# Second MLP product in blocks: four column blocks from eleven loads with one seven-product half, or from fourteen products

## The chip, the cores and the metric

One core of one Trainium2 chip. The metric is device microseconds for one execution of the whole program, the median of three runs. Weights lie in HBM as float32 and are read once or more per execution; activations stay in the core's SBUF.

## The reference

Two pre-norm residual layers over 256 tokens of width 2048: a Mamba-2 mixer in the first, dilated window attention in the second, and after each a squared-ReLU MLP of width 8192. A final RMSNorm ends it. The part that the change touches is the MLP:

```python
def sq_relu_mlp(h, w1, w2):
    a = jax.nn.relu(h @ w1)
    return (a * a) @ w2
...
        x = x + sq_relu_mlp(rms_norm(x, norm_mlp[i]), mlp_w1[i], mlp_w2[i])
```

## The kernel before, in words

Everything is float32 to the outside. TensorE (PE) is fed in a rounded type (fp32r), so each operand is carried as a high and a low part, and a product is made of three matmuls: high by high, high by low, low by high. Weights come in units of 128 x 2048 float32 (1 MB). For each unit `fetch` (L160) loads the raw tile on SP's queue (L174), ScalarE (ACT) writes the high part `wh` (L187), and VectorE (DVE) writes the low part `wl` as raw minus high (L188). This pair is called a split below. `unit_plan` writes the order of all units by hand; `take` hands a unit to the product that wants it and fetches ahead: `LOOKAHEAD = 3` units and three buffers each of raw, `wh` and `wl`. A buffer of `wh` is free again when PE has ended the unit three places before. Within the MLP each split is issued after the split of the unit before it in the plan.

The MLP works through the 8192 hidden columns in eight chunks of 1024 (`FC = 8`). A chunk has eight w1 units, U0 to U7, of 32 matmuls each (L215, tile names h). Each is evacuated: ACT copies half of the PSUM bank, DVE adds the other half, applies the ReLU with the norm's factor (L777), ACT squares and makes the high part, DVE the low part (L780). While chunk c+1's U units run, the products of chunk c with w2 run between them, in the order of `CHUNK_ORDER` (L69), for the first seven chunks of each layer:

- Output columns 0 to 1023 are made with seven block products instead of eight (P1 to P7, L812, 12 matmuls of 512 columns each; tile names px, pw, pz for their PSUM banks). Each needs a sum of up to four weight blocks and a sum of activation blocks. The weight sums grow in two scratch tiles, wa (P1, P5, P6, P4) and wb (P3, P7): the first block is loaded, each later one is added to the tile by a DMA that accumulates, issued on GpSimd's (POOL's) queue (L176). The activation sums are made by `combine` on DVE and split (L791, L792). After each product DVE adds the bank to the residual or subtracts it (L818).
- Output columns 1024 to 2047 are made plainly: four units D20, D21, D30, D31 of 24 matmuls each (L249 to L251), added to the residual on DVE (L256).

The last chunk of each layer is made plainly for all columns.

The order of instructions on PE is that of the plan in this stage. On the other engines and on the DMA queues a scheduler, called by the kernel, orders instructions by when they become ready on its own timeline, within the orders that the kernel gives. A transfer on SP's queue thus need not stand in the plan's order.

Of the kernel before, what the change touches and what calls it, by code (L numbers as in the profile page):

```python
# [8 lines left out]
F32 = mybir.dt.float32  # L9
# [29 lines left out]
LOOKAHEAD = 3  # L39
# [7 lines left out]
def unit_plan():  # L47
# [21 lines left out]
CHUNK_ORDER = ("U0 U1 P1 U2 P2 U3 U4 P5 D20 D21 P3 U5 U6 P6 U7 D30 P7 D31 P4").split()  # L69
# [3 lines left out]
WINOGRAD = {  # L73
    "P1": ("wa", 0, 0, True), "P2": ("raw", 1, 0, True), "P5": ("wa", 0, 1, False),
    "P3": ("wb", 1, 1, True), "P6": ("wa", 1, 1, False), "P7": ("wb", 0, 1, False),
    "P4": ("wa", 1, 0, False),
# [3 lines left out]
def mlp_plan(layer):  # L80
    plan = [("w1", layer, 0, u) for u in range(8)]
    for c in range(FC):
        if c + 1 < FC:
            for item in CHUNK_ORDER:
                if item[0] == "U":
                    plan.append(("w1", layer, c + 1, int(item[1])))
                elif item[0] == "P":
                    plan.append(("w2", layer, c, item))
                else:
                    plan.append(("w2", layer, c, int(item[1]), int(item[2])))  # L90
        else:
            plan += [("w2", layer, c, j, q) for j in range(4) for q in range(2)]
    return plan
# [3 lines left out]
def hybrid_trunk_kernel(ctx: ExitStack, tc: tile.TileContext, a: dict, out: bass.AP):  # L97
# [7 lines left out]

    def mm_bank(name):
        return psum.tile([P, 512], F32, tag="mm", name=name, bufs=4)

    def sm_bank(name):
        return psum.tile([P, 512], F32, tag="sm", name=name, bufs=4)  # L110
# [20 lines left out]
    mlp_pool, sums_of = [None], {}  # L131
# [3 lines left out]
    def source(u):  # L135
# [15 lines left out]
        if len(u) == 4:  # L151
            q, j = WINOGRAD[u[3]][1:3]
        else:
            j, q = u[3:]
        return a["w2"][((u[1] * FC + u[2]) * 4 + j) * 2 + q], 2048

    def fetch(i, ends=(16,)):

        src, n = source(plan[i])
        product = plan[i][3] if plan[i][0] == "w2" and len(plan[i]) == 4 else None  # L160
        where, _, _, begins = WINOGRAD.get(product, ("raw", 0, 0, True))
        if where == "raw":
            raw = wts.tile([P, 2048], F32, tag="raw", name=f"raw{i}", bufs=3)
        elif begins:
            raw = sums_of[where] = mlp_pool[0].tile([P, 2048], F32, tag=where, name=f"{where}{i}", bufs=1)
        else:
            raw = sums_of[where]
        wh = wts.tile([P, 2048], F32R, tag="wh", name=f"wh{i}", bufs=3)
        wl = wts.tile([P, 2048], F32R, tag="wl", name=f"wl{i}", bufs=3)
        ready[i] = (wh, wl)  # L170
        for k0, k1 in zip((0, *ends), ends):
            c = slice(k0 * n // 16, k1 * n // 16)
            if begins:
                load[i] = nc.sync.dma_start(raw[:, c], src[:, c]).ins  # L174
            else:
                nc.gpsimd.dma_start(raw[:, c], src[:, c], accum_op=ALU.add)  # L176
            with ExitStack() as order:
# [3 lines left out]
                if product == "P4":  # L181
# [10 lines left out]
    def take(*u):  # L192
# [9 lines left out]
    def cols_units(us, xs, names, cuts=(), first=False, between=None):  # L202
# [3 lines left out]
        banks = [mm_bank(name) for name in names]  # L206
# [24 lines left out]
    def cols_sum(ps, name):  # L231
        cross = work.tile([P, S], F32, tag="cross", name=name + "x", bufs=2)
        nc.scalar.activation(cross, ps[:, S:], AF.Copy)
        tot = work.tile([P, S], F32, tag="tot", name=name + "t", bufs=2)
# [91 lines left out]
    def ssm(nx):  # L326
        sp = ctx_ssm.enter_context(tc.tile_pool(name="ssm", bufs=1))
# [312 lines left out]
    def attention(xn, nx):  # L640
        ap = ctx_att.enter_context(tc.tile_pool(name="att", bufs=1))
# [110 lines left out]
    def mlp(layer, pool, xn, done):  # L752
# [9 lines left out]
        mlp_pool[0] = pool  # L762

# [4 lines left out]
        def chunk(c):  # L768
            act = pool.tile([P, 8, 2, S], F32R, tag="act", name=f"act{layer}_{c}", bufs=2)
            r = pool.tile([P, 8, S], F32, tag="r", name=f"r{layer}_{c}", bufs=1)  # L770
            return act, r

        def evacuate(c, u, ps, act, r):
            name = f"h{layer}_{c}_{u}"
            tot = cols_sum(ps, name)
            t = r[:, u]
            nc.vector.scalar_tensor_tensor(t, tot, 0.0, rb, op0=ALU.max, op1=ALU.mult)  # L777
            nc.scalar.activation(t, t, AF.Square)  # L778
            nc.scalar.activation(act[:, u, 0, :], t, AF.Copy)
            nc.vector.tensor_tensor(act[:, u, 1, :], t, act[:, u, 0, :].bitcast(F32), ALU.subtract)  # L780

        def combine(c, r):

            t1, t2 = slice(0, P), slice(P, S)
            a11, a12, a21, a22 = r[:, :4, t1], r[:, 4:, t1], r[:, :4, t2], r[:, 4:, t2]
            s = [pool.tile([P, 4, P], F32, tag="s", name=f"s{layer}_{c}_{k}", bufs=2) for k in range(2)]
            parts = {}

            def split(k, t):
                parts[k] = pool.tile([P, 4, 2, P], F32R, tag=f"s{k}", name=f"sp{layer}_{c}_{k}", bufs=1)  # L790
                nc.scalar.activation(parts[k][:, :, 0], t, AF.Copy)  # L791
                nc.vector.tensor_tensor(parts[k][:, :, 1], t, parts[k][:, :, 0].bitcast(F32), ALU.subtract)  # L792

            nc.vector.tensor_tensor(s[0], a21, a22, ALU.subtract)
            split(1, s[0])
            nc.vector.scalar_tensor_tensor(s[1], s[0], -1.0, a11, op0=ALU.mult, op1=ALU.subtract)
            split(2, s[1])
            s4 = pool.tile([P, 4, P], F32, tag="s", name=f"s{layer}_{c}_3", bufs=2)
            nc.vector.scalar_tensor_tensor(s4, a12, -1.0, s[1], op0=ALU.mult, op1=ALU.subtract)
            split(4, s4)  # L800
            s3 = pool.tile([P, 4, P], F32, tag="s", name=f"s{layer}_{c}_2", bufs=2)
            nc.vector.tensor_tensor(s3, a11, a21, ALU.add)
            split(3, s3)
            return parts
# [11 lines left out]
        def put(m, j, ps, op):  # L816
            xc = x_res[:, m, j * 512:(j + 1) * 512]
            nc.vector.tensor_tensor(xc, xc, ps, op)  # L818

        act, r = chunk(0)  # L820
        us, names = [("w1", layer, 0, u) for u in range(8)], [f"h{layer}_0_{u}" for u in range(8)]
        for u, ps in enumerate(cols_many(us, xs, names)):
            evacuate(0, u, ps, act, r)

        for c in range(FC - 1):
            parts = combine(c, r)
            act_next, r_next = chunk(c + 1)
            banks = {}

            def half(k0, t):  # L830
                return lambda i, part: act[:, k0 + i, part, t]

            t1, t2 = slice(0, P), slice(P, S)
            of = {"P1": half(0, t1), "P2": half(4, t1), "P4": half(4, t2)}
            for k, item in ((1, "P5"), (2, "P6"), (3, "P7"), (4, "P3")):
                of[item] = lambda i, part, k=k: parts[k][:, i, part]
            lhs = lambda k, part, t: act[:, k, part, t]
            for item in CHUNK_ORDER:
                if item[0] == "U":
                    u = int(item[1])  # L840
                    ps = in_order(lambda: cols_units([("w1", layer, c + 1, u)], xs,
                                                     [f"h{layer}_{c + 1}_{u}"], first=(u == 0))[0])
                    evacuate(c + 1, u, ps, act_next, r_next)
                elif item[0] == "D":
                    j, q = int(item[1]), int(item[2])
                    if q == 0:
                        banks[j] = [mm_bank(f"d{layer}_{c}_{j}_{m}") for m in range(NH)]
                    in_order(lambda: rows_unit(banks[j], [("w2", layer, c, j, q)], lhs, 4 * q, 4, 512,
                                               q == 0, q == 1))
                    if q == 1:  # L850
                        add_residual(banks[j], j)
                else:
                    where = {"P1": "x", "P6": "x", "P7": "x", "P4": "x", "P5": "w", "P3": "w",
                             "P2": "z"}[item]
                    first = where not in banks
                    if first:
                        banks[where] = sm_bank(f"p{where}{layer}_{c}")
                    product(c, item, banks[where], of[item], first)
                    for m, j, op in {"P1": [(0, 0, ALU.add)], "P2": [(0, 0, ALU.add)],
                                     "P5": [(1, 1, ALU.add)], "P3": [(0, 1, ALU.subtract)],  # L860
                                     "P6": [(0, 1, ALU.subtract)], "P7": [(1, 1, ALU.add)],
                                     "P4": [(1, 0, ALU.subtract)]}[item]:
                        put(m, j, banks[where], op)
            act, r = act_next, r_next

        c = FC - 1
        lhs = lambda k, part, t: act[:, k, part, t]
# [18 lines left out]
    with tc.tile_pool(name="mlp1", bufs=1) as pool:  # L886
# [5 lines left out]
        def gained(j):  # L892
            if j == 0:
                fin.append(pool.tile([P, D], F32, tag="wb", name="fin", bufs=1))
# [116 lines left out]
```

## Time and profile before

| | us |
|---|---|
| median of 3 runs (2599.93 to 2601.69) | 2600.74 |
| the profiled execution | 2599.4 |
| its span | 2597.6 |

| engine | busy us | share of the span |
|---|---|---|
| PE | 2582.3 | 99% |
| PE weight load (beside PE) | 2211.8 | 85% |
| DVE | 1878.7 | 72% |
| ACT | 1459.1 | 56% |
| POOL | 160.0 | 6% |

Busy times are shares of an average over stages; the seven chunk steps of each layer are one such stage. "DMA share" is the mean busy share of the core's 16 DMA engines in a stretch, and GB/s what they moved. The releaser behind an arrow (`<-`) is the instruction that ended an engine's idle time.

### The profile page before, as it was taken

To read this page: it belongs to the slowest core of one execution; us is meant where nothing else is said; L and a number is where in the kernel's file an instruction comes from. 1 tells how busy PE (TensorE), PEld (TensorE's weight loads), DVE (VectorE), ACT (ScalarE), POOL (GpSimd) and SP (SyncE) were. 2 spreads that over 40 slices of the span, in tenths; PEclk is the share of its full clock that TensorE was granted. 3 is DMA by queue.
4 is the path that set the end of the run, shared out by engine and by line. 5 is a ranking of instruction groups with operands and counts; after the bars stand their busy time and mean duration, and the time that the engine had idled before them with its cause. 6 is when DMAs were issued, how large, how long until landed. Compare 5 with 4: busy or idle time off the path is not lost.

```text
span 2597.6 us, 34416 instructions
## 1 busy us (share of the span) xinstructions
PE 2582.3 (99%) x13977; PEld 2211.8 (85%) x13977; DVE 1878.7 (72%) x2182; ACT 1459.1 (56%) x1774; POOL 160.0 (6%) x131
## 2 busy tenths in 40 slices
PE   9999999999999999999999999999999999999998
PEld 7888888888888888888888999998888888888887
DVE  7888688686677677777766666666667777677765
ACT  7675365464555555555546655656565555555554
POOL 0121021211000000000000000000000000000001
PEclk9999999999999999999999999999999999999999
DMA  7645555555577787778765454444457777877783
GB/s 284 209 169 193 191 195 180 180 191 187 191 222 232 236 231 239 229 235 234 231 195 183 166 175 162 159 158 165 168 209 216 234 237 235 232 230 239 228 241 131
DMA packets 79087, 533.88 MB, mean 206 GB/s; under 512 B 8784, under 2 KB 9424, under 8 KB 19536
## 3 DMA queue, kind: packets, MB, share of 16 engines
q1 hardware_dynamic: 68256, 462.86, 50.5%
q0 software_dynamic: 8064, 58.72, 12.5%
q10 hardware_dynamic: 2608, 10.09, 1.2%
q8 instruction: 110, 1.80, 0.3%
q14 instruction: 49, 0.40, 0.0%
HBM read 529.48 MB, written 2.16 MB: 205 GB/s over the span
## 4 chain that ended last, share of the span: by engine, by line
PE 95%; DVE 2%; ACT 1%; DMA 1%; POOL 1%; issue 1%; SPq 0%; ACTq 0%; POOLq 0%; DVEq 0%
PE h L215 28%; PE qk L215 10%; PE c L215 8%; PE px L812 6%; PE d L249 5%; PE d L250 5%; PE d L251 5%; PE pw L812 3%; PE wo L250 2%; PE wo L249 2%; PE wo L251 2%; PE z L250 2%; PE z L251 2%; PE z L249 2%; PE v L249 2%; PE v L251 2%
## 5 line engine op out<-in xcount | busy, mean ns | idle before, releaser
L188 DVE TENSOR_TENSOR wl<-raw,wh 128x2048 fp32r<-128x2048 f32 (+4 forms) x428 | 934.6, 2185 | 578.0 <-ACT wh L187 577.0
L187 ACT ACTIVATE wh<-raw 128x2048 fp32r<-128x2048 f32 (+4 forms) x428 | 782.7, 1831 | 640.8 <-PE h L215 216.5
L215 PE MATMUL h<-xn,wh 128*128 128x512 f32 x2048 | 715.9, 394 | 0.0
L215 PE MATMUL h<-xn,wl 128*128 128x256 f32 x2048 | 571.2, 280 | 0.0
L215 PEld LDWEIGHTS h<-xn,wh 128*128 128x128 f32 x2048 | 383.9, 188 | 87.0
L215 PEld LDWEIGHTS h<-xn,wl 128*128 128x128 f32 x2048 | 383.6, 187 | 4.2
L215 PE MATMUL c<-xn,wh 128*128 128x512 f32 x768 | 272.4, 397 | 2.5 <-ACT wh L187 2.3
L215 PE MATMUL qk<-xn,wh 128*128 128x512 f32 x768 | 271.1, 395 | 0.0
L251 PE MATMUL d<-wh,act 128*128 128x512 f32 x576 | 224.3, 390 | 0.0
L250 PE MATMUL d<-wl,act 128*128 128x512 f32 x576 | 223.9, 389 | 0.0
L249 PE MATMUL d<-wh,act 128*128 128x512 f32 x576 | 218.7, 390 | 0.0
L215 PE MATMUL qk<-xn,wl 128*128 128x256 f32 x768 | 216.7, 284 | 0.0
L215 PE MATMUL c<-xn,wl 128*128 128x256 f32 x768 | 215.0, 282 | 0.8 <-DVE wl L188 0.8
L215 PEld LDWEIGHTS c<-xn,wh 128*128 128x128 f32 x768 | 143.7, 188 | 37.2 <-ACT wh L187 4.4
L215 PEld LDWEIGHTS qk<-xn,wh 128*128 128x128 f32 x768 | 143.9, 188 | 30.2
L215 PEld LDWEIGHTS c<-xn,wl 128*128 128x128 f32 x768 | 143.9, 188 | 3.0 <-DVE wl L188 1.1
L215 PEld LDWEIGHTS qk<-xn,wl 128*128 128x128 f32 x768 | 143.7, 188 | 3.2 <-issue 2.7
L251 PEld LDWEIGHTS d<-wh,act 128*128 128x128 f32 x576 | 108.1, 188 | 22.6
L249 PEld LDWEIGHTS d<-wh,act 128*128 128x128 f32 x576 | 108.1, 188 | 22.3
L250 PEld LDWEIGHTS d<-wl,act 128*128 128x128 f32 x576 | 108.1, 188 | 22.0
L778 ACT ACTIVATE r<-r 128x256 f32<-128x256 f32 x128 | 52.2, 410 | 101.7 <-DVE r L777 101.7
L250 PE MATMUL z<-wl,xn 128*128 128x512 f32 x256 | 101.4, 396 | 0.3 <-DVE wl L188 0.3
(348 smaller groups left out, 4186.3 us busy)
## 6 DMA issues: line engine op xcount, KB each, us to landing
raw<-in_w SPq DMA_DIRECT2D x214, 1024.0 KB, 4.9
raw<-in_w_in SPq DMA_DIRECT2D x74, 1024.0 KB, 4.8
raw<-in_w_qk SPq DMA_DIRECT2D x48, 1024.0 KB, 4.8
wa<-in_w POOLq DMA_DIRECT2D x42, 1024.0 KB, 8.2
raw<-in_w_out SPq DMA_DIRECT2D x32, 1024.0 KB, 4.8
raw<-in_w_v SPq DMA_DIRECT2D x32, 768.0 KB, 4.3
wa<-in_w SPq DMA_DIRECT2D x14, 1024.0 KB, 4.8
wb<-in_w SPq DMA_DIRECT2D x14, 1024.0 KB, 5.0
```

Source lines behind the costliest of these rows:

```text
L187: high[i] = nc.scalar.activation(wh[:, c], raw[:, c], AF.Copy).ins
L188: low[i] = nc.vector.tensor_tensor(wl[:, c], raw[:, c], wh[:, c].bitcast(F32), ALU.subtract).ins
L215: latest[0] = nc.tensor.matmul(ps[:, :n], (wh, wl)[part][:, kt * P:(kt + 1) * P], xs[:, kt, :, :].rearrange("p a t -> p (a t)")[:, :n], st ...
L249: nc.tensor.matmul(banks[m][:, :n], hi, wh[:, c], start=st, stop=False)
L250: nc.tensor.matmul(banks[m][:, :n], hi, wl[:, c], start=False, stop=False)
L251: latest[0] = nc.tensor.matmul(banks[m][:, :n], lo, wh[:, c], start=False, stop=sp).ins
L778: nc.scalar.activation(t, t, AF.Square)
L812: latest[0] = nc.tensor.matmul(ps, lhs(i, part), w[:, n], start=(first and i == 0 and part == 0 and w is wh), stop=(i == 3 and part == 1), ...
```

## The change

Both column halves are made from seven products. The four D units of a chunk go, and the seven products exist twice, a for columns 0 to 1023 and b for columns 1024 to 2047: fourteen products beside the eight U units. The order keeps U units apart; products stand next to each other in places.

```diff
-CHUNK_ORDER = ("U0 U1 P1 U2 P2 U3 U4 P5 D20 D21 P3 U5 U6 P6 U7 D30 P7 D31 P4").split()
+CHUNK_ORDER = ("1a U0 1b U1 5a U2 5b 3a U3 3b U4 6a U5 6b 7a U6 7b 2a 4a U7 2b 4b").split()
...
+PRODUCTS = {
+    "1": ("A", 0, 0, "load"), "5": ("A", 0, 1, "add"), "6": ("A", 1, 1, "add"), "4": ("A", 1, 0, "sum"),
+    "3": ("B", 1, 1, "load"), "7": ("B", 0, 1, "add"), "2": ("raw", 1, 0, "load"),
 }
```

A and B are the weight scratches, now Aa, Ab, Ba, Bb. "load" is a plain load, "add" an accumulating DMA. Product 4 has no DMA of its own: the block of product 2 is loaded for product 2, and DVE adds it to A, 128 x 2048, before product 4's split.

```diff
+                if item and item[0] == "2":
+                    a = sums_of["A" + item[1]]
+                    nc.vector.tensor_tensor(a[:, c], a[:, c], raw[:, c], ALU.add)
```

Buffers are named one by one instead of drawn from pools of three or four; the least recently used one is taken. In the chunk steps there are four pairs of `wh` and `wl` (three elsewhere), two raw buffers (three elsewhere; the third is Aa), and the fetch runs as far ahead as a free pair allows, three units.

```diff
+    banks_of, raws, splits = Slots(8), Slots(3), Slots(4)
...
+    def split_slot(i):
+        return splits.peek(range(4 if chunked(i) else 3))
...
-        while cursor[1] < min(len(plan), i + LOOKAHEAD):
+        while cursor[1] < len(plan) and splits.user.get(split_slot(cursor[1]), -1) < i:
```

PSUM banks are named as well: U units use banks 0, 1 and 6; the products banks 2, 3, 4, 5 and 7. Products 1, 6, 7, 4 share a bank (x) and 5, 3 share one (w), so each must wait until DVE has read the one before; product 2b shares a bank with 3b. Product 2a keeps bank 7 over all seven chunks and is added to the residual once, in the last. Outside the MLP the two groups of four banks stay, each bank now taken in fixed rotation.

```diff
+        put = {"1": ("x", 0, 0, ALU.add), "6": ("x", 0, 1, ALU.subtract), "7": ("x", 1, 1, ALU.add),
+               "4": ("x", 1, 0, ALU.subtract), "5": ("w", 1, 1, ALU.add), "3": ("w", 0, 1, ALU.subtract),
+               "2": ("z", 0, 0, ALU.add)}
+        place = {"wa": 2, "wb": 3, "xa": 4, "xb": 5, "za": 7, "zb": 3}
```

The activation sums are the same four per chunk, in three scratches (one of them a constant tile used elsewhere), each split once and used for both halves; the high and low parts of the left upper block and of the lower half lie in tiles of their own (`a1`, `a2`). The right upper block is split only in the last chunk (`complete`). The two reads of a U bank have priority over other work. The descriptor memory of POOL's DMAs is set to 4096 bytes.

## Rows read from the trace of the kernel before

**Rows 1.** The page: busy time of the engines over the span, and the granted clock of PE in 40 slices.

```profile
PE 2582.3 (99%) x13977; PEld 2211.8 (85%) x13977; DVE 1878.7 (72%) x2182; ACT 1459.1 (56%) x1774; POOL 160.0 (6%) x131
...
PEclk9999999999999999999999999999999999999999
```

**Rows 2.** The page: the chain of work that ended last, shares of the span by engine.

```profile
PE 95%; DVE 2%; ACT 1%; DMA 1%; POOL 1%; issue 1%; SPq 0%; ACTq 0%; POOLq 0%; DVEq 0%
```

**Rows 3.** The chain of waits in order of time, one chunk step of each layer (start us, length us, what).

```profile
945.26 2.75 PE pw L812 x12
961.61 11.17 PE h L215 x64
972.78 2.75 PE px L812 x12
975.53 5.59 PE h L215 x32
...
1979.37 2.75 PE pw L812 x12
...
2064.98 2.75 PE pw L812 x12
```

**Rows 4.** Busy time of each engine in four successive chunk steps of the first layer, each from one P5 to the next (columns: PE, PE weight load, DVE, ACT, POOL, with instructions; granted clock; DMA share; GB/s).

```profile
859.65:945.26 85.61, 85.61 (x437) 72.91 (x437) 62.52 (x62) 46.79 (x48) 3.43 (x4) 1.00 0.79 234
945.26:1030.88 85.62, 85.62 (x438) 72.91 (x437) 62.53 (x62) 46.80 (x48) 3.45 (x4) 1.00 0.79 233
1030.88:1116.49 85.61, 85.61 (x437) 72.90 (x437) 62.53 (x62) 46.78 (x48) 3.45 (x4) 1.00 0.79 234
1116.49:1202.10 85.61, 85.61 (x437) 72.90 (x437) 62.53 (x62) 46.79 (x48) 3.45 (x4) 1.00 0.78 234
```

**Rows 5.** Groups of DVE and ACT instructions in one chunk step, 945.26 to 1030.88 (count | busy us, mean ns of one | idle before them and its releaser).

```profile
L188 DVE TENSOR_TENSOR wl<-raw,wh 128x2048 fp32r<-128x2048 f32 x13 | 29.8, 2291 | 20.5 <-ACT wh L187 20.5
L780 DVE TENSOR_TENSOR act<-r,act 128x256 fp32r<-128x256 f32 x8 | 3.3, 418 | 0.0
L792 DVE TENSOR_TENSOR sp<-s,sp 128x512 fp32r<-128x512 f32 x4 | 2.7, 685 | 0.0
L818 DVE TENSOR_TENSOR x_res<-x_res,px 128x512 f32<-128x512 f32 x4 | 2.7, 679 | 0.0
...
L187 ACT ACTIVATE wh<-raw 128x2048 fp32r<-128x2048 f32 x14 | 26.8, 1917 | 25.3 <-PE h L215 13.1 <-PE d L251 8.9 <-issue 2.9
```

**Rows 6.** One split and the product that it feeds: ACT's and DVE's rows from the timeline, PE's from the chain.

```profile
1033.66 1.92 ACT L187 ACTIVATE wh<-wb 128x2048 fp32r<-128x2048 f32 x1 [0.38 <-PE pw L812]
...
1036.22 2.28 DVE L188 TENSOR_TENSOR wl<-wb,wh 128x2048 fp32r<-128x2048 f32 x1
...
1044.51 2.72 PE pw L812 x12
```

**Rows 7.** The DMA view of the same chunk step as rows 5: queues (packets, MB, share of 16 engines' time).

```profile
q1 hardware_dynamic: 2160, 15.73, 51.9%
q0 software_dynamic: 574, 4.18, 26.8%
```

**Rows 8.** Transfers about one accumulating DMA: its issue on POOL, the issue of a load on SP, the time to landing of both, and that of a load with no accumulating DMA beside it, issued at 985.3.

```profile
1003.50 0.86 POOL L176 DMA_DIRECT2D wa<-in_w  x1 [36.38 <-DVE wl L188]
...
L174 SPq DMA_DIRECT2D raw<-in_w x1: 328/328/328, 1007.3 to 1007.3; - x1
...
wa<-in_w POOLq DMA_DIRECT2D x1, 1024.0 KB, 8.2
raw<-in_w SPq DMA_DIRECT2D x1, 1024.0 KB, 6.6
...
L174 SPq DMA_DIRECT2D raw<-in_w x1: 328/328/328, 985.3 to 985.3; - x1
DMA to landing us min/median/max: 4.7/4.7/4.7
```

**Rows 9.** Stretches of the same few us (columns as in rows 4).

```profile
1005.00:1007.00 2.00, 2.00 (x14) 1.74 (x13) 2.00 (x1) 0.71 (x2) 0.00 (x0) 1.00 0.90 131
1007.00:1008.50 1.50, 1.50 (x11) 1.32 (x10) 1.50 (x4) 0.00 (x0) 0.00 (x0) 1.00 1.13 235
1008.50:1011.00 2.50, 2.50 (x14) 2.04 (x13) 0.48 (x2) 2.41 (x3) 0.00 (x0) 1.00 0.93 213
1011.00:1013.00 2.00, 2.00 (x13) 1.74 (x12) 2.00 (x2) 1.97 (x3) 0.00 (x0) 1.00 1.01 426
```

**Rows 10.** Issues on SP's queue before the U0 that starts the next chunk step at 997.47 (start us, length us).

```profile
980.48 0.33 SPq L174 DMA_DIRECT2D wb<-in_w  x1
985.31 0.33 SPq L174 DMA_DIRECT2D raw<-in_w  x1
990.89 0.33 SPq L174 DMA_DIRECT2D wa<-in_w  x1
...
997.47 11.16 PE h L215 x64
```

**Rows 11.** Who waited for whom in the attention stage, 1400 to 1880 us, the rows in which PE's side waits longest (us in total, times, longest us).

```profile
PEld qk L215 <- issue: 2.7, 7, 0.4
PEld pv L732 <- ACT ka L699: 1.7, 7, 0.2
```

More of the change, by code (lines that the diff above doesn't have):

```diff
@@ L86, in mlp_plan @@
                     plan.append(("w1", layer, c + 1, int(item[1])))
-                elif item[0] == "P":
+                else:
                     plan.append(("w2", layer, c, item))
-                else:
-                    plan.append(("w2", layer, c, int(item[1]), int(item[2])))
         else:
@@ L104, in hybrid_trunk_kernel, with __init__, peek, use @@
     dram = ctx.enter_context(tc.tile_pool(name="dram", bufs=1, space=bass.MemoryType.DRAM))
+    class Slots:
+        def __init__(self, n):
+            self.order, self.user = list(range(n)), {}
+        def peek(self, among):
+            return next(k for k in self.order if k in among)
+        def use(self, k, i=None):
+            self.order.remove(k)
+            self.order.append(k)
+            self.user[k] = i
+            return k
+    banks_of, raws, splits = Slots(8), Slots(3), Slots(4)
+    def bank(name, among):
+        k = banks_of.use(banks_of.peek(among))
+        return psum.tile([P, 512], F32, tag=f"b{k}", name=name, bufs=1)
     def mm_bank(name):
-        return psum.tile([P, 512], F32, tag="mm", name=name, bufs=4)
+        return bank(name, range(4))
     def sm_bank(name):
-        return psum.tile([P, 512], F32, tag="sm", name=name, bufs=4)
+        return bank(name, range(4, 8))
     x_res = const.tile([P, NH, D], F32, name="x_res")
@@ L130, in hybrid_trunk_kernel @@
     ready, load, high, low = {}, {}, {}, {}
-    mlp_pool, sums_of = [None], {}
+    mlp_pool, sums_of, stage = [None], {}, [None]
     cursor = [0, 0]
@@ L155, in source, with chunked @@
         return a["w2"][((u[1] * FC + u[2]) * 4 + j) * 2 + q], 2048
+    def chunked(i):
+        return plan[i][0] == "w1" and plan[i][2] > 0 or plan[i][0] == "w2" and len(plan[i]) == 4
+    def split_slot(i):
+        return splits.peek(range(4 if chunked(i) else 3))
     def fetch(i, ends=(16,)):
         src, n = source(plan[i])
-        product = plan[i][3] if plan[i][0] == "w2" and len(plan[i]) == 4 else None
-        where, _, _, begins = WINOGRAD.get(product, ("raw", 0, 0, True))
+        item = plan[i][3] if plan[i][0] == "w2" and len(plan[i]) == 4 else None
+        where, _, _, how = PRODUCTS[item[0]] if item else ("raw", 0, 0, "load")
         if where == "raw":
-            raw = wts.tile([P, 2048], F32, tag="raw", name=f"raw{i}", bufs=3)
-        elif begins:
-            raw = sums_of[where] = mlp_pool[0].tile([P, 2048], F32, tag=where, name=f"{where}{i}", bufs=1)
-        else:
-            raw = sums_of[where]
-        wh = wts.tile([P, 2048], F32R, tag="wh", name=f"wh{i}", bufs=3)
-        wl = wts.tile([P, 2048], F32R, tag="wl", name=f"wl{i}", bufs=3)
+            k = raws.use(raws.peek(range(2 if chunked(i) else 3)))
+            raw = wts.tile([P, 2048], F32, tag=f"raw{k}", name=f"raw{i}", bufs=1)
+        elif how == "load":
+            if where + item[1] == "Aa":
+                pool, tag = wts, f"raw{raws.use(2)}"
+            else:
+                pool, tag = mlp_pool[0], where + item[1]
+            raw = pool.tile([P, 2048], F32, tag=tag, name=f"{where}{item[1]}{i}", bufs=1)
+        else:
+            raw = sums_of[where + item[1]]
+        if where != "raw":
+            sums_of[where + item[1]] = raw
+        k = splits.use(split_slot(i), i)
+        pool = wts if k < 3 else mlp_pool[0]
+        wh = pool.tile([P, 2048], F32R, tag=f"wh{k}", name=f"wh{i}", bufs=1)
+        wl = pool.tile([P, 2048], F32R, tag=f"wl{k}", name=f"wl{i}", bufs=1)
         ready[i] = (wh, wl)
@@ L172, in fetch @@
             c = slice(k0 * n // 16, k1 * n // 16)
-            if begins:
+            if how == "load":
                 load[i] = nc.sync.dma_start(raw[:, c], src[:, c]).ins
-            else:
+            elif how == "add":
                 nc.gpsimd.dma_start(raw[:, c], src[:, c], accum_op=ALU.add)
@@ L200, in take, with cols_units @@
         return ready.pop(i)
-    def cols_units(us, xs, names, cuts=(), first=False, between=None):
+    def cols_units(us, xs, names, cuts=(), first=False, between=None, made=None):
         ws = [take(*u) for u in us]
-        banks = [mm_bank(name) for name in names]
+        banks = made or [mm_bank(name) for name in names]
         ends = (0, *cuts, KT)
@@ L229, in cols_many, with cols_sum @@
             yield cols_units([u], xs, [name])[0]
-    def cols_sum(ps, name):
+    def cols_sum(ps, name, tot=None):
         cross = work.tile([P, S], F32, tag="cross", name=name + "x", bufs=2)
         nc.scalar.activation(cross, ps[:, S:], AF.Copy)
-        tot = work.tile([P, S], F32, tag="tot", name=name + "t", bufs=2)
+        if tot is None:
+            tot = stage[0].tile([P, S], F32, tag="tot", name=name + "t", bufs=2)
         nc.vector.tensor_tensor(tot, ps[:, :S], cross, ALU.add)
@@ L326, in ssm @@
     def ssm(nx):
-        sp = ctx_ssm.enter_context(tc.tile_pool(name="ssm", bufs=1))
+        sp = stage[0] = ctx_ssm.enter_context(tc.tile_pool(name="ssm", bufs=1))
         n0 = Normed(0)
@@ L640, in attention @@
     def attention(xn, nx):
-        ap = ctx_att.enter_context(tc.tile_pool(name="att", bufs=1))
+        ap = stage[0] = ctx_att.enter_context(tc.tile_pool(name="att", bufs=1))
         dist = ap.tile([P, 3, AG, P], F32, name="dist")
@@ L762, in mlp @@
         mlp_pool[0] = pool
+        left, right = slice(0, P), slice(P, S)
         def in_order(make):
@@ L766, in in_order @@
                 return make()
[L768 to L804, printed above, removed]
@@ L814, in product @@
                             stop=(i == 3 and part == 1), skip_group_check=True).ins
[L816 to L820, printed above, removed]
+        cur = Chunk(0)
         us, names = [("w1", layer, 0, u) for u in range(8)], [f"h{layer}_0_{u}" for u in range(8)]
         for u, ps in enumerate(cols_many(us, xs, names)):
-            evacuate(0, u, ps, act, r)
-        for c in range(FC - 1):
[L826 to L837, printed above, removed]
+            cur.evacuate(u, ps)
@@ L841, in mlp @@
[L841 to L863, printed above, removed]
@@ L864, in mlp @@
-            act, r = act_next, r_next
+                    u, name = int(item[1]), f"h{layer}_{c + 1}_{item[1]}"
+                    ps = in_order(lambda: cols_units([("w1", layer, c + 1, u)], xs, [name],
+                                                     made=[bank(name, (0, 1, 6))])[0])
+                    nxt.evacuate(u, ps)
+                    continue
+                key, m, j, op = put[item[0]]
+                key += item[1]
+                kept = key == "za"
+                first = item[0] in "15" or item[0] == "2" and not (kept and c > 0)
@@ L866, in mlp @@
+                if first:
+                    banks[key] = bank(f"p{key}{layer}_{c}", [place[key]])
+                product(c, item, banks[key], of[item[0]], first)
+                if not kept or c == FC - 2:
+                    j += 2 * (item[1] == "b")
+                    xc = x_res[:, m, j * 512:(j + 1) * 512]
+                    nc.vector.tensor_tensor(xc, xc, banks[key], op)
+            cur = nxt
         c = FC - 1
-        lhs = lambda k, part, t: act[:, k, part, t]
+        cur.complete()
```

68 lines of the change are left out of this document (58 added, 10 removed).

## The prediction

> **What bounds the kernel now.** I read the page's busy times first: PE 2582.3 of 2597.6 us, every other engine far below, the granted clock at 9 tenths or more, the upper level of 2.4 GHz, in all 40 slices [rows 1]. The chain of work that ended last agrees: 95% of it is PE [rows 2]. So time is won only by giving PE less to do, and lost by letting it wait. The chain in order of time shows one period per chunk step, the same in both layers: 945.26 to 1030.88 and 1979.37 to 2064.98, 85.6 us [rows 3]. The table by stretch shows that PE is busy for all of it, DVE for 62.5 us, ACT for 46.8 us, POOL for 3.45 us, the DMA engines for 0.79 of it [rows 4]. There is no PE wait to remove there; the question is what the three other servers do when PE's work shrinks and theirs grows.
>
> **PE's work.** A U unit takes 5.59 us, a seven-product block 2.75 us for 12 matmuls [rows 3]. A step has 8 units (44.7 us) and 7 x 12 + 4 x 24 = 180 product matmuls in the other 40.9 us, 0.2272 us each. After it has 14 x 12 = 168: 12 fewer, 2.73 us, and a step of 82.9 us. Seven steps in two layers: 14 x 2.73 = 38.2 us. First and last chunks keep their matmuls. If nothing waits, the profiled 2599.4 becomes 2561.2; the median shown lies 1.3 above that execution, so 2562.5.
>
> **DVE and ACT.** Splits per step go from 19 to 22. A split costs 2.29 on DVE and 1.92 on ACT [rows 5]. DVE also adds the block of product 2 to A twice: the rows show no in-place sum of this size, so I bound it by the one-operand-more-or-less neighbours of the same 2048 elements: 1.9 us (ACT's copy) to 2.3 (the split), and take 2.29 as it is the same two-input form. Residual updates go from 11 to 13 (fourteen products, 2a kept in its bank) at 0.68. Instructions overlap by some 0.06 at their ends: the 62 means of a step sum to 66.5 us, against 62.5 busy [rows 4, 5]. So DVE gains 3 x 2.22 + 2 x 2.22 + 2 x 0.62 = 12.3 and stands at 74.9 of 82.9 us, 90%; ACT gains 3 x 1.86 and stands at 52.4, 63%. Both fit over a step. The tight stretch is the one where products crowd, 6b to 5a of the next step: 10 products and 4 units, 49.8 us of PE, against 14 splits, 2 sums, 4 evacuations (3 x 0.42 each), 9 updates and the activation sums with their splits (8 x 0.685), 53.3 less 2.9 of overlap, 50.4 us of DVE. That is even, not over; the other stretch has 24.5 us of DVE in 33.1 of PE. What covers unevenness is the distance between split and use. Now a split starts when PE leaves the unit three before: ACT began wb's 0.38 us after its release, DVE ended at 1038.50, PE used it at 1044.51, 6.0 us later [rows 6]. With four pairs one more item lies between. The summing instruction of 2 stands before the split of 2 on DVE, 2.29 us in a distance of 11.1 (U6's neighbours 7a, U6, 7b). I charge nothing for DVE and ACT; if the cover were gone, a backlog of some 1.2 us per step is what the tight stretch could show (0.6 over, twice for orders that fit badly).
>
> **DMA.** A step has 15 loads and 4 accumulating DMAs now; after it, 14 loads (8 units, 1, 3 and 2 for both halves) and 6 accumulating ones (5, 6, 7). By the queues' shares a load holds the engines 51.9% x 85.62 / 15 = 2.96 us and an accumulating one 26.8% x 85.62 / 4 = 5.74 us [rows 7]: 67.4 us become 75.9 of 82.9, 92%. That is the resource nearest to full, and what a load costs beside an accumulating DMA matters. The wa issued at 1003.50 took 8.2 us; a load issued at 1007.3 took 6.6, against 4.7 alone [rows 8]. While wa was in flight the engines moved 131 to 235 GB/s, and 426 from 1011.0 on [rows 9]: the load got next to nothing until wa was through, then its 1.05 MB in 2.5 us. So I treat the engines as one server, first come first served: 5.8 per accumulating DMA, 2.55 per load in a crowd, 1.4 from issue to first data, 1 at the end.
>
> Laid out so, with 0 at the start of 1a: each accumulating DMA is released by the split before it on its scratch. 1a's split may start when PE leaves 4a, at -11.1 (U7, 2b, 4b follow); with 4.2 us of split and 2.6 of queue on DVE, 5a is issued at -4.3. 5b, 6a, 6b, 7a follow at 2.8, 12.9, 18.6, 21.2, and the loads of U2, U3, U4, U5 at -1, 5.6, 15.5, 24.3, as the two raw tiles come free. Five accumulating DMAs and four loads, 39.2 us, run almost without a gap from -2.8 to 37: U5 lands at 37.9, is split by 42.4, and PE reaches it after 1a, 1b, 5a, 5b, 3a, 3b, 6a (19.2) and U0 to U4 (28.0) at 47.2. **4.8 us to spare**, the least of any transfer. The rest of the step is slack. The bounds: by the loads' share (2.96) and 6.3 for an accumulating DMA the same nine take 43.3 and U5 is late by nothing to 1.2 us; by 5.0 and 2.5 there are 9 us to spare. I take the middle, so no wait.
>
> The Trainium skill, "DMA: Bandwidth & Descriptors", section "SWDGE vs HWDGE vs iDMA", says that each DMA engine goes round robin between the queue of software descriptors and that of hardware ones. Rows 8 and 9 show a load that is held until the accumulating one is through, so here the trace speaks against it; by that rule U5 would share with 7a and land some 3 us sooner, and the sum would stay as it is.
>
> **Order and small things.** The layout leans on SP issuing by readiness: before, wb's load for the next step's P3 went out at 980.48, ahead of two raw loads and of wa and long before U0 [rows 10], though the plan has it later. So 3a and 3b should go out in the empty end of the step. Waits of products for DVE's reading of their shared bank: the nearest reuse (5a then 3a, 6a then 7a, 4b then 1b) has 8.3 us between, for an update of 0.68; nothing. U banks are three, with 16.6 us and more until reuse. POOL issues six at 0.86. The last chunk's extra split (`complete`, 0.6 on each engine) has 2.75 us of PE beside it. Named banks in the mixers can only add waits: PE's side waits 2.7 us in all of attention for its largest cause [rows 11]. I bound it by 0.5 us in each of 8 groups and 8 head pairs, 8 us, and by nothing, and take nothing since neither stage is touched otherwise.
>
> **Rivals.**
> *Partly eaten (0.12).* DMA or DVE comes out at its upper bound: 1.2 us per step, so 14 x 1.53 = 21 us won, 2579; with the mixers' 8 us, 2587. For it: 92% and 90%. Against: both bounds are ends, and the layout's slack is 4.8.
> *Eaten in full (0.05).* Waits of 2.4 to 3.1 us per step by the same causes: 2595 to 2606.
> *DMA becomes the bound (0.09), slower.* If SP issues in the plan's order, 3a's and 3b's loads (5.1) and 7b's accumulating DMA (5.8) stand before U5's load instead of behind it: 10.9 more, 6.1 past the slack; the step is 89.0 us, 14 x 3.4 = 47 us more, 2648. It decides from 4.8 + 2.73 = 7.5 us put in front of U5 on. For it: six accumulating DMAs fall in half a step. Against: rows 10.
> *It does not do what it says (0.02):* product matmuls at more than 0.2272 us, since 14 blocks switch banks 14 times. P blocks take 2.72 to 2.75 [rows 3, 6], so at most 14 x 0.02 per step, 4 us in all.
>
> **How the numbers follow.** The forecast, 2562.5 with a microsecond or so for the first step of each layer, 2563, has 0.72. Its own range is 2558 to 2571 (the 8 us of the mixers above, bank and clock luck below). About 0.2% (5 us) is what a measurement can tell from no change. Faster (below 2595.5): the forecast, the partial rival and the last one, 0.86, less 0.03 for what I have not seen, 0.83. Within 0.2%: the gain eaten in full, 0.05, and 0.01 of the unseen, 0.06. Slower: the DMA rival's 0.09 and the rest of it, 0.11. The range that leaves out 2 in 10 reaches over the partial rival: 2557 to 2592.
>
> **What would show it.** Steps of 82.9 us from 1a to 1a with PE busy throughout; 22 splits and two 2048-wide sums per step on DVE, at 75 us busy; DMA share near 0.9, with accumulating DMAs landing in 8 to 14 us where they queue; no row in which PE waits for `wl` of a U unit. PE waiting for U5's `wl` or its load, once a step, would make the DMA rival right; waits scattered over 2a, 4a, U7 would make DVE the cause; gaps in SSM or attention, the named banks. A step longer than 83.5 us or a time over 2592 makes the prediction wrong.

## The result and the profile after

The changed kernel takes 2564.67 us in the median of four runs (2563.86 to 2565.06), against 2600.34 for the kernel before: a ratio of 0.9863, with a 95% interval of 0.9846 to 0.9880. The forecast was 2563, its range 2557 to 2592. The profiled execution took 2564.77 with a span of 2562.8, 34.8 less than the span before.

Of the page of the changed kernel, busy times and the chain by engine, the rows that answer to [rows 1, 2]:

```profile
PE 2546.1 (99%) x13809; PEld 2180.0 (85%) x13809; DVE 2038.0 (80%) x2284; ACT 1521.1 (59%) x1814; POOL 186.7 (7%) x159
PEclk9999999999999999999999999999999999999999
...
PE 96%; DVE 1%; ACT 1%; DMA 1%; issue 0%; POOL 0%; SPq 0%; ACTq 0%; POOLq 0%; DVEq 0%
```

PE has 168 matmuls less (13977 to 13809), as counted: 12 in each of 14 steps. It is still busy for 99% of the span and is 96% of the chain. DVE went from 72% to 80%.

Two successive chunk steps of the first layer, U7 to U7 (columns as in [rows 4], which they answer), and 83 us of the same stage cut into the crowded and the loose part:

```profile
898.26:981.24 82.98, 82.98 (x425) 70.64 (x425) 73.64 (x70) 51.45 (x51) 5.19 (x6) 1.00 0.85 254
981.24:1064.23 82.99, 82.99 (x426) 70.65 (x425) 73.65 (x70) 51.34 (x51) 5.18 (x6) 1.00 0.85 253
...
881.00:933.00 52.00, 52.00 (x266) 44.21 (x265) 50.30 (x46) 32.27 (x30) 4.33 (x5) 1.00 0.88 263
933.00:964.00 31.00, 31.00 (x162) 26.44 (x161) 23.35 (x25) 19.19 (x21) 0.86 (x1) 1.00 0.82 236
```

A step is 2.62 us shorter and PE is never idle in it. Fourteen steps make 36.7 us. The span gained 34.8, since the stages outside lost some: by the chain the first MLP starts at 697.49, 2.8 us later than before, and 0.9 came back around the attention stage. The last two rows are the ones to remember: in the crowded part DVE is busy for 50.3 of 52.0 us, in the loose part for 23.4 of 31.0. (The expectation of f1 gives DVE 2.5 us of idle time in the crowded part; by the row it is 1.7.)

The DMA view of the step 898.26 to 981.24, the counterpart of [rows 7, 8]: SP's queue (q1) and POOL's (q0), then issues (KB each, median us to landing), then three issues on SP's queue:

```profile
q1 hardware_dynamic: 2022, 14.73, 47.6%
q0 software_dynamic: 864, 6.29, 37.4%
...
raw<-in_w SPq DMA_DIRECT2D x10, 1024.0 KB, 6.6
...
Ab<-in_w POOLq DMA_DIRECT2D x2, 1024.0 KB, 9.6
...
Bb<-in_w POOLq DMA_DIRECT2D x1, 1024.0 KB, 12.3
Ba<-in_w SPq DMA_DIRECT2D x1, 1024.0 KB, 4.8
```

```profile
903.07 0.33 SPq L207 DMA_DIRECT2D Ab<-in_w  x1
...
957.86 0.33 SPq L207 DMA_DIRECT2D Ba<-in_w  x1
...
966.19 0.33 SPq L207 DMA_DIRECT2D Bb<-in_w  x1
```

The accumulating DMAs queue, as forecast: some 10 to 12 us where they follow each other, against 8.2 [rows 8]. The loads of 3a and 3b (Ba, Bb) go out behind the last of them, that of 1b (Ab) just ahead of the first; all three land in 4.8 to 4.9 us, as if alone.

The six issues on POOL; U5's split, on ACT and on DVE; and from the chain 1a's product and the unit U5:

```profile
905.54 0.86 POOL L209 DMA_DIRECT2D Aa<-in_w  x1 [48.87 <-DVE wl L224]
912.87 0.86 POOL L209 DMA_DIRECT2D Ab<-in_w  x1 [6.47 <-DVE wl L224]
918.47 0.86 POOL L209 DMA_DIRECT2D Aa<-in_w  x1 [4.74 <-DVE wl L224]
927.31 0.87 POOL L209 DMA_DIRECT2D Ab<-in_w  x1 [7.97 <-DVE wl L224]
931.50 0.86 POOL L209 DMA_DIRECT2D Ba<-in_w  x1 [3.32 <-DVE wl L224]
938.79 0.86 POOL L209 DMA_DIRECT2D Bb<-in_w  x1 [6.43 <-DVE wl L224]
...
946.07 1.92 ACT L223 ACTIVATE wh<-raw 128x2048 fp32r<-128x2048 f32 x1 [3.11 <-DMA raw<-in_w]
...
948.02 2.29 DVE L224 TENSOR_TENSOR wl<-raw,wh 128x2048 fp32r<-128x2048 f32 x1 [2.65 <-ACT wh L223]
...
909.31 2.72 PE pxa L873 x12
...
956.42 5.59 PE h L251 x32
```

From 1a's start that is -3.8, 3.6, 9.2, 18.0, 22.2 and 29.5; the layout had -4.3, 2.8, 12.9, 18.6 and 21.2 for the first five. U5's load is what its split waits for (`<-DMA raw`): the split begins at 36.8, where the layout had the load land at 37.9, and ends at 950.31, 6.1 us before PE needs it.

### The profile page after: what moved, and what is told of

Same layout as the page of the kernel before. It is cut to its first block, busy times and chain, and to the rows that moved or that the text cites. A ratio compares the mean times of both kernels' runs of the same rounds, so it can differ in the third digit from the quotient of the medians.

```text
span 2562.8 us, 34291 instructions
## 1 busy us (share of the span) xinstructions
PE 2546.1 (99%) x13809; PEld 2180.0 (85%) x13809; DVE 2038.0 (80%) x2284; ACT 1521.1 (59%) x1814; POOL 186.7 (7%) x159
## 3 DMA queue, kind: packets, MB, share of 16 engines
q0 software_dynamic: 12096, 88.09, 17.3%
## 4 chain that ended last, share of the span: by engine, by line
PE 96%; DVE 1%; ACT 1%; DMA 1%; issue 0%; POOL 0%; SPq 0%; ACTq 0%; POOLq 0%; DVEq 0%
PE h L251 28%; PE qk L251 11%; PE c L251 9%; PE pxb L873 6%; PE pxa L873 6%; PE pwb L873 3%; PE pwa L873 3%; PE wo L287 2%; PE wo L286 2%; PE wo L288 2%; PE z L286 2%; PE z L288 2%; PE z L287 2%; PE v L286 2%; PE v L288 2%; PE v L287 2%
## 5 line engine op out<-in xcount | busy, mean ns | idle before, releaser
L224 DVE TENSOR_TENSOR wl<-raw,wh 128x2048 fp32r<-128x2048 f32 (+4 forms) x386 | 839.6, 2177 | 338.0 <-ACT wh L223 335.5
L223 ACT ACTIVATE wh<-raw 128x2048 fp32r<-128x2048 f32 (+4 forms) x386 | 702.2, 1821 | 442.9 <-PE h L251 92.4
L223 ACT ACTIVATE wh<-Ab 128x2048 fp32r<-128x2048 f32 x42 | 80.5, 1916 | 70.3 <-DMA Ab<-in_w 51.3
L224 DVE TENSOR_TENSOR wl<-Ab,wh 128x2048 fp32r<-128x2048 f32 x42 | 96.1, 2288 | 12.7 <-ACT wh L223 12.7
L223 ACT ACTIVATE wh<-Aa 128x2048 fp32r<-128x2048 f32 x42 | 80.4, 1914 | 36.7 <-DMA Aa<-in_w 28.4
L286 PE MATMUL z<-wh,xn 128*128 128x512 f32 x256 | 101.5, 397 | 0.0
L288 PE MATMUL z<-wh,xn 128*128 128x512 f32 x256 | 101.1, 395 | 0.0
L224 DVE TENSOR_TENSOR wl<-Aa,wh 128x2048 fp32r<-128x2048 f32 x42 | 96.0, 2287 | 5.2 <-ACT wh L223 5.0
L286 PE MATMUL wo<-wh,y3t 128*128 128x512 f32 x256 | 100.1, 392 | 0.0
```

The source lines that it names most:

```text
L223: high[i] = nc.scalar.activation(wh[:, c], raw[:, c], AF.Copy).ins
L224: low[i] = nc.vector.tensor_tensor(wl[:, c], raw[:, c], wh[:, c].bitcast(F32), ALU.subtract).ins
L286: nc.tensor.matmul(banks[m][:, :n], hi, wh[:, c], start=st, stop=False)
L288: latest[0] = nc.tensor.matmul(banks[m][:, :n], lo, wh[:, c], start=False, stop=sp).ins
```

## The experiments

Twelve further kernels. All but f4 ran once, so their times carry the spread of single runs: the four of the changed kernel lie within 1.2 us, the four of the kernel before within 3.3. The kernel before took 2599.94 us beside the first eight and 2599.75 in the median beside the last four. Figures "a step" that are not read from a row divide the difference to the profiled 2564.77 by 14.

**e1, the loads in the plan's order.**

```diff
-                load[i] = nc.sync.dma_start(raw[:, c], src[:, c]).ins
+                with ExitStack() as queued:
+                    if chunked(i) and i - 1 in last_load:
+                        queued.enter_context(tc.issue_after(last_load[i - 1]))
+                    load[i] = nc.sync.dma_start(raw[:, c], src[:, c]).ins
...
```

> Loads of the chunk steps go out on SP in the plan's order instead of by readiness; nothing else changes. One-server theory (accumulating DMAs 5.8 us, loads 2.55 us, first come first served): the loads of 3a and 3b (5.1 us) move into the half step with the six accumulating DMAs, in front of U5's load, whose split now ends 6 us before PE needs it; 7a's and 7b's accumulating DMAs start later too. Steps of 85 to 87 us instead of 82.99, total 2593 to 2621. The rival of the prediction, with 7b in front as well: 89.0 us, 2648. Round-robin theory (a load shares with an accumulating DMA packet by packet): steps stay at 83.0, total 2565.

2602.14 us: the gain is gone, 2.67 us a step, 85.7 on average; the single steps take 83.4 to 89.5. One of them, 2a to 2a (columns as above), then DMA issues over two steps, then the chain in the same step:

```profile
896.24:981.86 85.62, 83.59 (x426) 70.61 (x425) 73.70 (x70) 51.07 (x51) 5.20 (x6) 1.00 0.81 247
```

```profile
raw<-in_w SPq DMA_DIRECT2D x20, 1024.0 KB, 8.8
...
Ba<-in_w SPq DMA_DIRECT2D x2, 1024.0 KB, 18.4
Bb<-in_w SPq DMA_DIRECT2D x2, 1024.0 KB, 20.8
```

```profile
929.44 20.21 DMA raw<-in_w
...
954.03 5.68 PE h L257 x31
959.71 2.76 PE pxa L879 x12
```

The same transfers, a lower DMA share, and PE waits 2.0 us in this step. The loads of 3a and 3b take 18 to 21 us, not 4.8: they now run beside the accumulating DMAs. The load that PE waits for stands behind them on SP's queue and takes 20.2 us; it is that of U4, the unit ahead of 6a (pxa), and not that of U5. Over the twelve steps from 2a to 2a that the trace holds, PE waits for 23 us and its matmuls take 13 us longer, most of it in the steps with a granted clock of 0.96 to 0.98.

The time lies in the range of the one-server theory, but the transfers do not follow its rule. From 940 to 950 us accumulating DMAs and loads are both in flight (queue: packets, MB, share):

```profile
q0 software_dynamic: 189, 1.42, 68.3%
q1 hardware_dynamic: 188, 1.40, 34.8%
```

The two queues move the same, packet for packet. First come, first served does not hold: the load of 3a, issued at 911.94, landed at 930.48, later than the accumulating DMA issued at 916.30, which landed at 929.92. So the transfers go as the round-robin theory has it; that the step would then stay at 83.0 us had not been worked out and was wrong. The prediction's own price for the rival, 89.0, was too high.

**e2, product 4's block by an accumulating DMA instead of DVE.**

```diff
-... "4": ("A", 1, 0, "sum"),
+... "4": ("A", 1, 0, "acc"),
...
-            elif how == "add":
+            elif how in ("add", "acc"):
...
-                if item and item[0] == "2":
-                    a = sums_of["A" + item[1]]
-                    nc.vector.tensor_tensor(a[:, c], a[:, c], raw[:, c], ALU.add)
...
```

> Product 4's block is added by an accumulating DMA again, as before the change, and not by DVE: 8 accumulating DMAs and 14 loads a step, two 2048-wide sums less on DVE (4.4 us). One-server theory: 8 x 5.8 + 14 x 2.55 = 82.1 us of DMA in a step of 83.0, so gaps and the crowding of six in half a step show: steps of 84 to 88 us, total 2579 to 2635, DMA share 0.95 or more. If DVE were the nearer bound: steps stay at 83.0 with DVE near 69 us busy, total 2565.

2563.39 us, and no change in the step (one step; then POOL's queue over three):

```profile
898.00:981.00 83.00, 83.00 (x426) 70.65 (x425) 69.15 (x68) 52.15 (x51) 6.90 (x8) 1.00 0.96 279
...
q0 software_dynamic: 3456, 25.17, 50.5%
```

The DMA engines are busy for 0.96 of the step and PE waits for none of it. The expectation of 84 to 88 fell: the sum of 82.1 was nearly right, but the transfers left hardly a gap. One costs less here: 50.5% of 249 us for 24 accumulating DMAs is 5.24 us each, not 5.8. So the DMA engines were not the nearest bound of the changed kernel, as long as the order is right.

**e3 and e4, more work for DVE.** The low part is written twice for 5a and 7b, and for 1a, 5a, 3a, 6a, 7a, 2a.

```diff
+                if item in ('5a', '7b'):
+                    low[i] = nc.vector.tensor_tensor(wl[:, c], raw[:, c], wh[:, c].bitcast(F32),
+                                                     ALU.subtract).ins
```

> The low part of the splits of 5a and 7b is written twice: two more 2048-wide DVE instructions a step, 73.65 + 4.44 = 78.1 us of DVE in 82.99. Theory that DVE has 9 us of room a step and that splits are ready some 4 to 6 us ahead: steps stay within 0.3 us of 83.0, total 2565 to 2569. Theory that DVE is the near bound in the crowded stretch: one us or more a step, 2579 or above.

> The low part of six splits a step (1a, 5a, 3a, 6a, 7a, 2a) is written twice: 73.65 + 6 x 2.22 = 87.0 us of DVE in a step of 82.99, so DVE must be the bound. Steps of 87.0 us if DVE then never idles, up to 90 if it still waits for ACT's high parts some 3 us a step: total 2621 to 2663, and PE waits for wl in the chain. A step under 86.5 would mean that a DVE instruction costs less than its row says.

2630.76 and 2701.43 us: 4.7 and 9.8 us a step for 4.4 and 13.3 us of DVE. The first refutes the 9 us of room, though DVE would have been idle for 4.9 us of the old step. What PE waits for in it is not the split that was made longer but `sp`, the split activation sum of product 5, at 5a (bank w, pwa):

```profile
PE pwa L876 <- DVE sp L852: 24.6, 12, 2.8
PE pwa L876 <- ACT sp L851: 17.3, 12, 2.5
```

That the cost comes near the length of the two instructions is chance, as f1 shows. e4 missed its range (2621 to 2663): a step of 92.7 on average, longer than the 87.0 of DVE's sum and the 90 allowed for. DVE is idle for 24 of 300 us, PE waits for `wl` before products, and the granted clock is 0.97:

```profile
900.00:1200.00 300.00, 276.94 (x1344) 230.09 (x1343) 275.54 (x239) 161.95 (x158) 15.54 (x18) 0.97 0.75 223
```

**f1 and f2, where the instructions are put.** The same edit for 7b alone, and for 3b and 6a.

> The low part of 7b's split alone is written twice: one more DVE instruction of 2.22 us a step, in the crowded stretch 6b to 5a. In the profile after DVE works there from 881 to 933 us with 2.5 us of idle time in all. Theory that this stretch is the nearest bound and full: steps of 84.5 to 85.3 us, 21 to 32 us more in all, 2586 to 2597. Theory that the two instructions of the earlier run hurt only because the one at 5a lies on the chain load, split, accumulating DMA, split of Aa: steps of 83.0, 2565.

> The low parts of 3b's and 6a's splits are written twice: the same two more DVE instructions a step as in the run with 5a and 7b, but worked off while PE is in the loose stretch U2 to U5. Theory that the crowded stretch alone is full: steps within 0.4 us of 83.0, total 2565 to 2570. Theory that DVE's sum over the step decides (78.1 us with its waits for ACT): as with 5a and 7b, 87.7 us a step, 2631. A figure between would mean that 6a's split or 6b's accumulating DMA is late.

f2 took 2564.80 us: two more instructions a step for nothing, with DVE at 78.1 us.

```profile
898.00:981.00 83.00, 83.00 (x425) 70.65 (x424) 78.01 (x72) 50.87 (x51) 5.19 (x6) 1.00 0.87 254
```

f1 took 2627.07: one instruction of 2.2 us in the crowded part costs 4.45 us a step over the 14, more than either theory gave and nearly what two cost in e3. Two of the 62 us lie ahead of the first MLP; the rest falls on the twelve steps with another chunk step behind them, 87.97 us each. Two steps of f1, 2a to 2a, and what PE waits for:

```profile
988.46:1074.96 86.50, 83.54 (x425) 70.56 (x425) 75.73 (x71) 51.22 (x52) 5.18 (x6) 1.00 0.83 243
1074.96:1163.23 88.27, 85.16 (x425) 71.77 (x425) 75.83 (x71) 50.97 (x52) 5.17 (x6) 0.98 0.83 238
```

```profile
PE pwa L876 <- DVE sp L852: 20.1, 12, 1.7
PE pwa L876 <- ACT sp L851: 17.7, 12, 1.8
```

PE waits some 3 us in each of them, always before 5a, and as in e3 not for a weight split but for `sp`. ACT's timeline shows why. First the changed kernel, then f1, both just before 5a:

```profile
916.03 0.62 ACT L848 ACTIVATE sp<-ssq_junk 128x512 fp32r<-128x512 f32 x1
...
922.62 1.92 ACT L223 ACTIVATE wh<-Ab 128x2048 fp32r<-128x2048 f32 x1 [2.90 <-DMA Ab<-in_w]
```

```profile
1107.05 1.91 ACT L223 ACTIVATE wh<-Ab 128x2048 fp32r<-128x2048 f32 x1 [3.92 <-DVE s L858]
1108.86 0.61 ACT L851 ACTIVATE sp<-ssq_junk 128x512 fp32r<-128x512 f32 x1
```

In the changed kernel `sp` is copied at 916.03, before 5b's split (`wh<-Ab`), and PE starts 5a at 925.95. In f1 DVE came to the sum later, 11.1 us behind 1a's start and not 6.0, the copy stands behind 5b's split, ACT idled 3.9 us ahead of that split, and `sp` was late. The releaser named there is DVE's `s`, but Ab's accumulating DMA, issued at 1097.73, took 9.2 us and landed at 1106.94, within 0.1 us of the same moment; one step earlier the chain itself names it (`1011.24 9.05 DMA Ab<-in_w`). So it is an order on ACT that costs the wait, with ACT idle for 3.9 us and then DVE, waiting for ACT, for 2.0. The rest is longer matmuls. In three of the twelve steps the granted clock is 1.00 and PE is busy for 83.5 to 83.6 us; in nine it is 0.96 to 0.98 and PE is busy for 85.1 to 85.9. In one of the nine:

```profile
1102.50:1112.00 9.50, 6.39 (x36) 4.98 (x34) 7.48 (x9) 5.58 (x7) 1.28 (x2) 0.99 1.04 279
1112.00:1117.00 5.00, 5.00 (x17) 4.06 (x18) 5.00 (x6) 1.60 (x3) 1.30 (x2) 0.67 0.99 272
1117.00:1122.00 5.00, 5.00 (x29) 4.34 (x29) 4.32 (x7) 1.86 (x3) 0.00 (x0) 1.00 1.01 210
```

After PE was idle for 3.1 of 9.5 us, the granted clock is 0.67 on average over the next 5 us, part of it at the lower level of 1.2 GHz, and back at 1.00 after. That step has 85.16 us of PE busy time for work that takes 82.99, 2.2 us more; the other step shown, with 2.96 us of idle time, has only 0.55 more.

**f3, e2 and e3 together.**

> 5a's and 7b's low parts written twice as in the run that took 2630.8, and product 4's block added by an accumulating DMA instead of DVE (the run that took 2563.4): DVE has as much to do in the crowded stretch as in the changed kernel. Theory that DVE's work in that stretch was what cost 4.7 us a step: steps of 83.0 to 83.6, total 2563 to 2573. Theory that the late accumulating DMA of 6a or 6b was: the DMA engines are fuller now (share 0.96), so 87 us a step or more, 2625 and above.

2564.05 us: the two instructions that cost 66 us cost nothing once the two sums of product 2 are off DVE. So it was DVE's load in the crowded part that brought the wait on, not a late DMA; the DMA engines are at 0.97 and 0.98 here. One of the steps:

```profile
898.00:981.00 83.00, 83.00 (x426) 70.66 (x426) 74.48 (x70) 52.08 (x51) 6.91 (x8) 1.00 0.98 281
```

**e5, three pairs of `wh` and `wl`.**

```diff
-        return splits.peek(range(4 if chunked(i) else 3))
+        return splits.peek(range(3))
```

> Three pairs of wh and wl in the chunk steps instead of four: a split starts when PE leaves the unit three before, not four before. Theory that the fourth pair is what lets splits run ahead through the crowded stretch: PE waits some 1 to 2 us a step, mostly where a split is only two products away from its use (U0, U1, U7 with neighbours 2b 4b 1a, 2a 4a), steps of 84 to 85 us, total 2579 to 2594. Rival, the fourth pair is spare: steps stay at 83.0, total 2565.

2566.16 us, the steps 83.00 with PE busy throughout: the fourth pair is spare, and my expectation of 84 to 85 fell. The extra 1.4 us lie ahead of the first MLP, which starts 1.2 us later.

```profile
815.00:898.00 83.00, 83.00 (x426) 70.66 (x425) 73.77 (x70) 51.23 (x50) 5.16 (x6) 1.00 0.86 254
```

**e6, units in pairs.** The plan reads `1a U0 U1 1b 5a 5b U2 U3 3a 3b U4 U5 6a 6b 7a U6 U7 7b 2a 4a 2b 4b`.

> Order of the plan 1a U0 U1 1b 5a 5b U2 U3 3a 3b U4 U5 6a 6b 7a U6 U7 7b 2a 4a 2b 4b: units stand in pairs, products in threes to six. Six products in a row, 7b to 1a, are 16.5 us of PE against 6 splits, 2 sums, 6 updates and most of the activation sums on DVE, some 24 us; with splits only three ahead PE must wait there. Theory that keeping units apart is worth something: 1 to 3 us a step, 2579 to 2607. Rival, that the order is free as long as the sum over a step fits: 83.0, 2565.

2578.22 us, 0.96 us a step, just below the least that was expected. PE waits for the low part of 5b (8.2 us in 10 waits over the run), and in the chain what stands before it is Ab's accumulating DMA; most of the rest is matmuls that take 0.3 to 0.4 us longer a step, 1.8 in one. Against this one other order, keeping units apart is worth 13 of the 36 us.

**e7 and e8, the banks.** In e7 the kernel before names its eight banks in fixed rotation, in the two groups of four. In e8 the changed kernel draws the mixers' banks from pools that are opened for each stage and closed after it.

> The kernel before with PSUM banks named in fixed rotation, least recently used first, instead of drawn from two pools of four; nothing else of the change. The profile after shows the first MLP's first matmul 2.8 us later than before (697.49 against 694.69), 2 us of it in the first SSM group, where PE waits for the norm's factor by way of ACT. Theory that fixed banks cause it: this kernel starts its first MLP at 696.7 to 697.5 and takes 2602 to 2604. Rival, that another part does (the sums' tile in another pool, the smaller descriptor memory, instruction placement): start at 694.7, total 2600.

> The changed kernel with the banks of the SSM and attention stages drawn from two pools of four again, named banks in the MLPs only. Theory that fixed banks cost the 2.8 us of the SSM stage: first MLP from 694.7 to 695.5, total 2562 to 2563. Rival, another part: 697.5 and 2565.

e7 took 2601.63 us, 1.7 more than the run beside it, within the spread of single runs and a little under the 2602 expected. The trace decides: its first MLP starts at 697.68 (694.69 before), as late as in the changed kernel, so fixed rotation is the cause of the later start. e8 took 2590.28, far from either theory: its steps are 83 us, but at the three changes of pools PE waits 5.4, 3.4 and 4.1 us for the norm's factor, and the first MLP starts only at 703.99, so it says nothing on the total. The first SSM group, 120 to 140 us, in the kernel before, the changed one, e7 and e8, in this order:

```profile
120.00:140.00 20.00, 19.28 (x120) 15.59 (x119) 15.86 (x18) 13.62 (x18) 11.12 (x7) 1.00 0.61 201
```

```profile
120.00:140.00 20.00, 17.26 (x77) 13.24 (x76) 16.93 (x17) 12.90 (x16) 13.52 (x7) 1.00 0.57 201
```

```profile
120.00:140.00 20.00, 17.61 (x73) 13.57 (x72) 16.39 (x16) 13.21 (x16) 13.44 (x7) 0.93 0.56 205
```

```profile
120.00:140.00 20.00, 19.30 (x119) 15.54 (x119) 15.87 (x19) 12.74 (x17) 11.12 (x7) 1.00 0.58 203
```

Named banks leave PE busy for 17.3 to 17.6 us of these 20, drawn ones for 19.3.

**f4, all banks drawn from two pools of four.**

```diff
-        return psum.tile([P, 512], F32, tag=f"b{k}", name=name, bufs=1)
+        tag = "mm" if k in (0, 1, 3, 6) and len(among) != 4 or among == range(4) else "sm"
+        return psum.tile([P, 512], F32, tag=tag, name=name, bufs=4)
```

> The changed kernel with all PSUM banks drawn from two pools of four again: U units and the b products of bank w and z from one, the other products from the other; the mixers as before the change. Theory that the fixed rotation costs the SSM stage 2.8 us and nothing in the MLP needs it: first MLP from 694.5 to 695, steps of 83.0, total 2562 (ratio to before 0.985). If the draw gives U units only two free banks at times: steps of 83.0 still, or PE waiting for a U bank's reading, 84 and 2579.

2562.77 us (median of four, 2562.09 to 2563.07), a ratio of 0.9856 (0.9839 to 0.9872); the first MLP starts at 695.00. Its runs lie below all those of the changed kernel (lowest 2563.86), by 1.9 us in the median, though the intervals of the two ratios overlap; the profile has 2.5 us of it ahead of the MLP. It is the fastest version seen.

## Why the prediction was right, and where its steps were not

- **PE's work and the chain.** Right to 0.1 us a step: 12 matmuls fewer, 82.9 forecast, 82.99 measured, PE never idle. This term is the whole of the gain. The product matmuls take 0.2279 us each ((82.99 - 44.7) / 168) instead of 0.2272, 1.5 us over the fourteen steps; the last rival gave bank switches up to 4 us for that, and whether they are the cause is not shown.
- **DVE and ACT.** Their sums were a little high: 74.9 and 52.4 forecast, 73.65 and 51.3 measured. The sum of A and the block was priced right, 2.29, as the split's two-input form. The tight stretch was found and called even (50.4 of 49.8). Cut as the prediction cuts it, 6b to 5a on PE (879.01 to 928.70), DVE is busy for 46.1 of 49.7 us; it is fullest from 881 to 933, 50.3 of 52.0. The step that failed is the one behind it: that four pairs and the distance to use give cover, so that a 0.6 us overrun would cost about 1.2. The fourth pair covers nothing measurable (e5), and 2.2 us more in that stretch cost 4.45 (f1), by an order on ACT that the sum of DVE's work does not show. The forecast held because the stretch just fits in the order that was made for it. How much room another order of ACT would leave is not shown.
- **DMA.** The share came out at 0.86, not 0.92: a transfer held the engines for less than before, 5.2 us for an accumulating one (37.4% of 82.98 us / 6) and 2.8 for a load. The model of one server, first come first served, gave the issues within 1.0 us but for 6a's (3.7), and U5's spare time as 4.8 against 6.1. Its bound was mis-added: 43.3 us is 4.1 more than 39.2, which leaves 0.7 of the 4.8 to spare and not 1.2 too late, and no row shows the 6.3 in it. DMA was called the resource nearest to full; by e2 and f3 it takes two more accumulating DMAs a step for nothing, while DVE in the crowded part took not one more instruction without a wait (f1). The nearest edge was misnamed.
- **One server.** [Rows 8, 9] were read too far. The load of 1007.3 does get nothing at first: from 1007.3 to 1010 only POOL's queue moved packets. Likewise a load of the changed kernel, issued at 908.04, moved none until 911.9. But where both queues have had work for longer they share: 53 packets each from 926 to 929 in the changed kernel, 189 and 188 from 940 to 950 in e1. This agrees with what the Trainium skill says in "DMA: Bandwidth & Descriptors", section "SWDGE vs HWDGE vs iDMA", that a DMA engine goes round robin between the queue of software descriptors and that of hardware ones. That first come, first served came so near to the issue times is then luck, at least in part; why a load first moves nothing for three to four us is open.
- **Order.** SP does issue by readiness, and that is worth as much as the whole change: e1 loses 37.4 us. The rival was right that the loads of 3a and 3b would hold up a unit's load, but its price (89.0, 2648) was too high by 46 us: it had 10.9 us more in front of U5, while PE waits for U4, some 2 us a step.
- **Named banks.** Taken at nothing, bounded at 8 us; they cost 2.5 to 3.0 (f4, e7), all of it in the first SSM group and before. How much varies: with the same named banks the first MLP starts at 696.2 in e2 and at 699.5 in f1. With this the forecast for the profiled execution, 2561.2, would have been 2564, against 2564.8 measured; the matmuls' 1.5 less the 0.9 around attention make up the rest.

## What to carry to other kernels

Balance a stretch, not a stage: an engine busy for 89% of a step was busy for 97% of 52 us of it, and one instruction put there cost more than its length while two in the loose part were free. Ask of each transfer which half of the step it falls in: the order of the loads was worth 37 us, two more accumulating DMAs a step cost nothing. When a wait is priced, look at what a late instruction makes the scheduler put in front of another: here one copy behind another on ACT put a DMA's wait in front of PE.

## What the hardware showed that I had not expected

The DMA engines ran at a share of 0.96 to 0.98 and 276 to 281 GB/s with PE waiting for nothing (e2, f3). Beside an accumulating DMA a load of 1 MB moved nothing for its first three to four us, and then shared packet for packet (changed kernel, e1). A wait of some 3 us on PE was followed by a granted clock at the lower level in nine steps of f1 and not in three others with waits as long, 2.1 to 2.9 us of longer matmuls against some 0.6: over the twelve steps 38 us of waits became 60.
